# Hybrid decoder trunk: weight sums of the feed-forward by accumulating transfers, three plain tiles, and four smaller edits

## Chip, cores and metric

The kernel runs on one core of a Trainium2 chip. The metric is the device time of one execution in microseconds (us). Before the change the median of 3 runs is 1248.66 us, from 1247.74 to 1249.43. PE is the matrix engine (its weight loads are listed as PEld), DVE the vector engine, ACT the scalar engine, POOL the GpSimd engine, and SP the queue that issues nearly all DMA transfers.

## The reference

Two layers, each an attention part of three head groups followed by a SwiGLU feed-forward, on 512 tokens of width 1024 with a hidden width of 2816:

```python
for l in range(DEPTH):
    h = rms_norm(x, attn_norm[l])
    proj = h @ w_in[l]
    ...                       # forgetting, differential and top-k sparse attention
    x = x + concatenate([o_fox, o_diff, o_dsa]) @ w_out[l]
    h = rms_norm(x, ffn_norm[l])
    gate, up = split(h @ w_gate_up[l], 2)
    x = x + (silu(gate) * up) @ w_down[l]
```

All inputs and outputs are float32.

## The kernel before

Activations are kept transposed: eight tiles `x[m]` of 128 features by 512 tokens. Every large product is made of three matrix passes: each operand is split into a rounded part `h` (written by ACT) and a remainder `lo` (written by DVE, in the projections of attention mostly by POOL), and `mm3` (lines 165 to 168) adds h*h, lo*h and h*lo. So PE never reads a raw weight: SP loads it, ACT rounds it, DVE subtracts, and only then PE starts.

The feed-forward (`feed_forward`, line 936) handles the hidden width in 22 tiles of 128 columns, `f` = 0 to 21. For `f` below `DIRECT` (4) a tile is plain: gate and up are each eight k-tiles by three passes of 512 columns, 48 matmuls. From `f` = 4 on a tile goes through `seven` (line 1026): the 2 by 2 block product of gate and up against the two halves of the tokens and of the features, by seven instead of eight half-size products (Winograd's form), 7 x 4 x 3 = 84 matmuls of 256 columns. Its products run in the order a11, T2, T3, T1, a12, T4, 22; the second ones on a bank (a12, T4, 22) add to what the first ones left there, so DVE or ACT must have read the bank before. For it `input_sums` (line 994) makes sums of the normalized input's quarters once a layer, and each tile needs four sums of weight quarters, `ws_f_0` to `ws_f_3`, which DVE makes (lines 1036 to 1039) from two raw tiles of 512 KB. `split_sum` (line 1017) then splits each sum, `whole` the three quarters that are used as they are. The sums and the temporaries of `input_sums` share one ring of five buffers (tag `ws`); the split sums have rings of five each. `down` (line 1086) follows after f = 7, f = 14 and at the end.

The order of PE's work is the order in which the code is written. The other engines' order is set by a scheduler with the priorities of `AHEAD`, and each engine then runs its list strictly in that order; so an instruction that waits holds up everything behind it on its engine. POOL has no work in the feed-forward.

Outside the feed-forward the change touches `key_stacks` (line 423), which makes the two stacked transposes of a key's rounded part and remainder on PE, with an ACT copy each; the first load (line 112); and the last add and store of `down` (lines 1095 to 1097).

Of the kernel before, what the change touches and what calls it, by code (L numbers as in the profile page):

```python
# [11 lines left out]
F32 = mybir.dt.float32  # L12
F32R = mybir.dt.float32r
AF = mybir.ActivationFunctionType
ALU = mybir.AluOpType
AX = mybir.AxisListType

P = 128
S = 512
NB = S // P  # L20
D = 1024
KT = D // P
DEPTH = 2
# [3 lines left out]
NF = FF // P  # L27
# [28 lines left out]


VALUES = [4, 4, 2, 4, 4, 2]
DIRECT = 4
GH = 8  # L60
POFF = (0, 512, 896, 1152)

# [24 lines left out]
def trunk(ctx: ExitStack, tc: tile.TileContext, x_in, w_in, w_out, w_gu, w_dn, vecs, gfeat, rope, out):  # L87
    nc = tc.nc
    V, A, G, T, SY = nc.vector, nc.scalar, nc.gpsimd, nc.tensor, nc.sync
# [4 lines left out]
    small = ctx.enter_context(tc.tile_pool(name="small", bufs=2))  # L94
# [11 lines left out]
    f32 = lambda ap: ap.bitcast(F32)  # L106
# [2 lines left out]

    x = [main.tile([P, S], F32, name=f"x{m}") for m in range(KT)]  # L110
    gf = const.tile([P, gfeat.shape[1]], F32, name="gf")
    SY.dma_start(gf, gfeat)


    ident = const.tile([P, P], F32, name="ident")
# [105 lines left out]
    def attention(l, ap):  # L221
# [189 lines left out]
        def stacked(src, name, tag="qk", bufs=5):  # L411

            ps = st_tile(f"tp_{name}", F32R)
            for b in range(NB):
                T.transpose(ps[:, b * P:(b + 1) * P], src(b), identr)
            dst = ap.tile([P, S], F32R, tag=tag, name=f"T_{name}", bufs=bufs)
            with ahead("stack"):
                A.activation(dst, ps, AF.Copy)
            return dst

        flat = lambda a: a.rearrange("p t e -> p (t e)")

        def key_stacks(hl, name, tag="qk", bufs=5):

            return [stacked(lambda b: flat(hl(b))[:, 64 * e:64 * e + 128], f"{name}{e}", tag, bufs) for e in range(2)]


        def scores(blocks, q, k, bias, p, stat, name):
# [289 lines left out]
        raws, hl, rr, outs, lows = {}, {}, {}, {}, {}  # L718
# [169 lines left out]
        q = index_queries(0)  # L888
        for h in range(IDX):
            if h == 1:  # L890
                skT = key_stacks(lambda b: hlk[:, b, 1], f"sk{l}", "skT", 2)
            step(filler, int(INDEX_FILL[4 * h + 1]))
            nq = index_queries(h + 1) if h + 1 < IDX else None
            for i in range(1, NB):
                step(filler, int(INDEX_FILL[4 * h + 1 + i]))
                index_score(h, q, i)
            q = nq
# [38 lines left out]
    def feed_forward(l, fp):  # L936
# [3 lines left out]
        y = split_input(l, 1, range(KT))  # L940
        acc = square_sum(fp, f"1{l}", (("gh", GH), ("gl", GH)))
        R = fp.tile([P, S], F32, tag="R", name=f"R{l}")
        half = KT // 2 * P
        H = S // 2

# [46 lines left out]
        Y = {}  # L992

        def input_sums(kt):
            xg = []
            for m in (kt, kt + KT // 2):
                t = fp.tile([P, S], F32, tag="ws", name=f"xg{l}_{m}", bufs=5)
                A.activation(t, x[m], AF.Copy, scale=gf[:, (2 * l + 1) * KT + m:(2 * l + 1) * KT + m + 1])
                xg.append(t)
            b11, b12, b21, b22 = (t[:, o:o + H] for t in xg for o in (0, H))  # L1000
            ta, tb = (fp.tile([P, S], F32, tag="ws", name=f"t{i}{l}_{kt}", bufs=5) for i in "ab")
            t1, t3, t2, t4 = (t[:, o:o + H] for t in (ta, tb) for o in (0, H))
            V.tensor_tensor(t1, b12, b11, op=ALU.subtract)
            V.tensor_tensor(t3, b22, b12, op=ALU.subtract)
            V.tensor_tensor(t2, b22, t1, op=ALU.subtract)
            V.tensor_tensor(t4, b21, t2, op=ALU.subtract)
            Y[kt] = {k: [t[:, o:o + H] for t in y[m]] for k, m, o in
                     (("11", kt, 0), ("21", kt + KT // 2, 0), ("22", kt + KT // 2, H))}
            for src, name, ks in ((ta, "s", ("T1", "T3")), (tb, "t", ("T2", "T4"))):
                h = fp.tile([P, S], F32R, tag=f"Yh{name}{kt}", name=f"Yh{l}_{name}{kt}")  # L1010
                A.activation(h, src, AF.Copy)
                lo = fp.tile([P, S], F32R, tag=f"Yl{name}{kt}", name=f"Yl{l}_{name}{kt}")
                V.tensor_tensor(lo, src, f32(h), op=ALU.subtract)
                for i, k in enumerate(ks):
                    Y[kt][k] = [t[:, i * H:(i + 1) * H] for t in (h, lo)]
# [10 lines left out]
        def seven(f):  # L1026

            raws, parts = [], {}
            for u in range(2):
                raw = (fp if u else wp).tile([P, 1024], F32, tag="raw", name=f"raw_gu{l}_{f}_{u}", bufs=2)  # L1030
                SY.dma_start(raw, w_gu[l, :, (2 * f + u) * KT * P:(2 * f + u + 1) * KT * P])
                raws.append(raw)
            a11, a12, a21, a22 = (r[:, o:o + half] for r in raws for o in (0, half))
            sums = [fp.tile([P, half], F32, tag="ws", name=f"ws{l}_{f}_{i}", bufs=5) for i in range(4)]
            with ahead("fh"):
                V.tensor_tensor(sums[0], a21, a22, op=ALU.add)
                V.tensor_tensor(sums[1], sums[0], a11, op=ALU.subtract)
                V.tensor_tensor(sums[2], a11, a21, op=ALU.subtract)
                V.tensor_tensor(sums[3], a12, sums[1], op=ALU.subtract)

            def whole(src, k):
                h = wp.tile([P, 512], F32R, tag="wh", name=f"wh_gu{l}_{f}_{k}")
                with ahead("fh"):
                    A.activation(h, src, AF.Copy)
                lo = wp.tile([P, 512], F32R, tag="wl", name=f"wl_gu{l}_{f}_{k}")
                with ahead("fl"):
                    V.tensor_tensor(lo, src, f32(h), op=ALU.subtract)
                return h, lo

            def product(ps, w, k, first, last):  # L1050
                for kt in range(KT // 2):
                    cs = slice(kt * P, (kt + 1) * P)
                    mm3(ps, w[0][:, cs], w[1][:, cs], *Y[kt][k], first and kt == 0, last and kt == KT // 2 - 1)

            a, c = (mm_tile(f"gu{l}_{f}_{k}")[:, :H] for k in "ac")
            b, d = (st_tile(f"gu{l}_{f}_{k}")[:, :H] for k in "bd")
            gs, us = pair(f)
            u2 = fp.tile([P, H], F32, tag="u2", name=f"u2{l}_{f}", bufs=2)
            product(a, whole(a11, "a"), "11", True, True)
            with ahead("post"):  # L1060
                A.activation(u2, a, AF.Copy)
            product(b, split_sum(sums[1], f"{l}_{f}_1", V), "T2", True, True)
            with ahead("post"):
                V.tensor_tensor(u2, b, u2, op=ALU.add)
            product(d, split_sum(sums[2], f"{l}_{f}_2", V), "T3", True, True)
            with ahead("post"):
                V.tensor_tensor(us[:, H:], d, u2, op=ALU.add)
            product(c, split_sum(sums[0], f"{l}_{f}_0", V), "T1", True, True)
            with ahead("post"):
                V.tensor_tensor(us[:, H:], c, us[:, H:], op=ALU.add)  # L1070
            product(a, whole(a12, "b"), "21", False, True)
            with ahead("post"):
                V.tensor_tensor(gs[:, :H], a, R[:, :H], op=ALU.mult)
            product(d, whole(a22, "d"), "T4", False, True)
            with ahead("post"):
                V.tensor_tensor(us[:, :H], d, u2, op=ALU.add)
            V.tensor_tensor(us, us, R, op=ALU.mult)
            product(c, split_sum(sums[3], f"{l}_{f}_3", V), "22", False, True)
            with ahead("post"):
                V.tensor_tensor(gs[:, H:], c, u2, op=ALU.add)  # L1080
            V.tensor_tensor(gs[:, H:], gs[:, H:], R[:, H:], op=ALU.mult)
            A.activation(gs, gs, AF.Silu)
            V.tensor_tensor(us, us, gs, op=ALU.mult)
            inner(f, us)

        def down(group, ms):
            f0, f1 = DOWN_GROUPS[group]
            n = (f1 - f0) * P
            for m in ms:
                off = KT * P * f0 + m * n  # L1090
                part = weights(w_dn[l, :, off:off + n], n, P, f"dn{l}_{f0}_{m}", low="fl")
                ps = mm_tile(f"dn{l}_{f0}_{m}")
                for e, f in enumerate(range(f0, f1)):
                    mm3(ps, *part(e * P, (e + 1) * P), gt[f][0], gt[f][1], f == f0, f == f1 - 1)
                V.tensor_tensor(x[m], ps, x[m], op=ALU.add)  # L1095
                if l == DEPTH - 1 and f1 == NF:
                    SY.dma_start(out[:, m, :], x[m])

        def norm_row():
            rows = st_tile(f"rrow{l}")  # L1100
# [96 lines left out]
```

## Time and profile before

| | |
|---|---|
| median of 3 runs | 1248.66 us |
| the profiled execution's own time | 1247.4 us |
| its span, first to last instruction | 1245.7 us |
| PE busy / DVE busy / ACT busy / POOL busy | 99% / 80% / 60% / 21% |
| PE's share of the chain that ended last | 91% |
| mean granted clock of PE | 1.00 |
| feed-forward of layer 0 / layer 1 | about 278 to 616 us / 895 to 1242 us |

Busy shares are means over stages with different limits: in the tiles of the seven-product form PE and DVE are both full, in `down` DVE has room. The profile lists each instruction's start and duration; neighbouring instructions of one engine overlap, so the cost of one in a full row of them is the distance between two starts, not its duration.

### The profile page before, as it was taken

The numbers are of one execution on the slowest core, as the hardware profiler recorded it, in microseconds if no ns is written. First come the engines' busy times: TensorE is split into PE (matmuls) and PEld (weight loads), VectorE is DVE, ScalarE is ACT, GpSimd is POOL, SyncE is SP. The second block draws the span as 40 slices with busy tenths as digits, with TensorE's granted clock in tenths as the row PEclk, the third lists the DMA queues.
The fourth block names the chain that finished last, engine by engine and source line by source line (L and its number), as shares of the span: only waits on it lengthen the run. The fifth ranks groups of instructions, "written<-read, shape, count | busy, mean of one in ns | idle before, by whom it ended". The sixth has DMA issues, their size and how long they took to land.

```text
span 1245.7 us, 22873 instructions
## 1 busy us (share of the span) xinstructions
PE 1230.3 (99%) x8366; PEld 1112.1 (89%) x8366; DVE 1001.2 (80%) x2345; ACT 741.9 (60%) x1686; POOL 262.2 (21%) x379
## 2 busy tenths in 40 slices
PE   9999999999999999999999899999999999999998
PEld 9988897887998998999899888978789989989997
DVE  5689987879976995998545999868799679959962
ACT  6678778867543552554457787888675335534531
POOL 2554566320000000000026635653200000000000
PEclk9999999999999999999999999999999999999999
DMA  5221221133423332422332312211333243234232
GB/s 191 86 77 52 77 74 35 57 109 102 117 77 112 116 99 81 130 85 69 98 89 69 94 52 60 74 47 52 119 102 114 77 131 102 82 99 125 75 97 83
DMA packets 34640, 111.77 MB, mean 90 GB/s; under 512 B 3952, under 2 KB 4448, under 8 KB 34528
## 3 DMA queue, kind: packets, MB, share of 16 engines
q1 hardware_dynamic: 34528, 110.31, 29.7%
q8 instruction: 66, 1.08, 0.4%
q14 instruction: 46, 0.38, 0.1%
HBM read 108.14 MB, written 2.15 MB: 89 GB/s over the span
## 4 chain that ended last, share of the span: by engine, by line
PE 91%; DVE 5%; ACT 3%; issue 0%; DMA 0%; SPq 0%; ACTq 0%; DVEq 0%
PE dn L168 7%; PE dn L167 6%; PE dn L166 6%; PE pj L166 6%; PE pj L168 6%; PE pj L167 6%; PE gu_d L166 3%; PE gu_a L166 3%; PE gu_a L167 3%; PE gu_d L168 3%; PE gu_a L168 3%; PE gu_d L167 3%; PE gu_c L166 3%; PE gu_c L167 3%; PE gu_c L168 3%; PE gu L166 2%
## 5 line engine op out<-in xcount | busy, mean ns | idle before, releaser
L166 PE MATMUL pj<-wh_in,yh 128*128 128x256 f32 (+1 forms) x704 | 201.8, 287 | 1.3 <-ACT wh_in L151 1.3
L168 PE MATMUL pj<-wl_in,yh 128*128 128x256 f32 (+1 forms) x704 | 198.5, 282 | 0.2 <-DVE wl_in L156 0.2
L167 PE MATMUL pj<-wh_in,yl 128*128 128x256 f32 (+1 forms) x704 | 198.4, 282 | 0.0
L151 ACT ACTIVATE wh_dn<-raw_dn 128x512 fp32r<-128x512 f32 x96 | 57.1, 595 | 138.6 <-PE dn L168 106.3
L168 PE MATMUL dn<-gl,wh_dn 128*128 128x512 f32 x352 | 138.7, 394 | 0.0
L167 PE MATMUL dn<-gh,wl_dn 128*128 128x512 f32 x352 | 138.0, 392 | 0.0
L166 PEld LDWEIGHTS pj<-wh_in,yh 128*128 128x128 f32 x704 | 134.3, 191 | 4.0 <-issue 1.9
L166 PE MATMUL dn<-gh,wh_dn 128*128 128x512 f32 x352 | 136.6, 388 | 0.0
L167 PEld LDWEIGHTS pj<-wh_in,yl 128*128 128x128 f32 x704 | 134.4, 191 | 0.7
L168 PEld LDWEIGHTS pj<-wl_in,yh 128*128 128x128 f32 x704 | 134.4, 191 | 0.4 <-DVE wl_in L156 0.4
L156 POOL TENSOR_TENSOR wl_in<-raw_in,wh_in 128x256 fp32r<-128x256 f32 x144 | 107.5, 774 | 112.3 <-ACT wh_in L151 85.0
L1020 ACT ACTIVATE wsh<-ws 128x512 fp32r<-128x512 f32 x144 | 89.5, 630 | 68.8 <-PE gu_c L168 29.3
L156 DVE TENSOR_TENSOR wl_dn<-raw_dn,wh_dn 128x512 fp32r<-128x512 f32 x96 | 61.6, 645 | 49.6 <-ACT wh_dn L151 49.0
L1023 DVE TENSOR_TENSOR wsl<-ws,wsh 128x512 fp32r<-128x512 f32 x144 | 97.6, 684 | 0.7
L167 PEld LDWEIGHTS dn<-gh,wl_dn 128*128 128x128 f32 x352 | 66.1, 188 | 15.2
L166 PEld LDWEIGHTS dn<-gh,wh_dn 128*128 128x128 f32 x352 | 66.1, 188 | 14.5
L168 PEld LDWEIGHTS dn<-gl,wh_dn 128*128 128x128 f32 x352 | 66.2, 188 | 13.1
L231 POOL MEMSET causal<- 128x512 f32 x2 | 1.1, 527 | 357.8 <-PE dn L168 357.8
L1095 DVE TENSOR_TENSOR x<-dn,x 128x512 f32<-128x512 f32 x48 | 32.8, 690 | 43.8 <-PE dn L168 43.7
L151 ACT ACTIVATE wh_in<-raw_in 128x512 fp32r<-128x512 f32 (+1 forms) x88 | 53.4, 623 | 20.8 <-PE pj L167 11.4
L880 DVE MAX8 top<-sc 128x8 f32<-128x384 f32 (+2 forms) x96 | 51.7, 547 | 0.3
L881 DVE MATCH_REPLACE8 sc<-top,sc 128x384 f32<-128x384 f32 (+2 forms) x96 | 51.5, 538 | 0.0
(397 smaller groups left out, 3935.6 us busy)
## 6 DMA issues: line engine op xcount, KB each, us to landing
raw_gu<-in_w_gu SPq DMA_DIRECT2D x88, 512.0 KB
raw_in<-in_w_in SPq DMA_DIRECT2D x39, 512.0 KB
raw_dn<-in_w_dn SPq DMA_DIRECT2D x32, 448.0 KB
raw_dn<-in_w_dn SPq DMA_DIRECT2D x16, 512.0 KB
cr<-rtd_c SPq DMA_DIRECT2D x12, 256.0 KB
raw_o_fox<-in_w_out SPq DMA_DIRECT2D x8, 384.0 KB
x<-in_x_in SPq DMA_DIRECT2D x8, 256.0 KB
raw_o_diff<-in_w_out SPq DMA_DIRECT2D x4, 512.0 KB
```

The source lines that it names most:

```text
L151: A.activation(h[:, :w], raw[:, o:o + w], AF.Copy)
L156: eng.tensor_tensor(lo[:, a:e], raw[:, o + a:o + e], f32(h[:, a:e]), op=ALU.subtract)
L166: T.matmul(ps, ah, bh, start=first, stop=False, skip_group_check=True)
L167: T.matmul(ps, al, bh, start=False, stop=False, skip_group_check=True)
L168: T.matmul(ps, ah, bl, start=False, stop=last, skip_group_check=True)
L231: G.memset(causal, 0.0)
L880: V.max(top, sc[i])
L881: V.match_replace(sc[i], top, sc[i], TAKEN)
L1020: A.activation(h, src, AF.Copy)
L1023: eng.tensor_tensor(lo, src, f32(h), op=ALU.subtract)
L1095: V.tensor_tensor(x[m], ps, x[m], op=ALU.add)
```

## The change

Six edits in one.

1. `DIRECT` is 3: tile f = 3 of each layer goes through `seven` too.
2. In `seven`, `ws_f_0` (a21 + a22) and `ws_f_2` (now a11 + a21) are made by the DMA engines: POOL issues a plain load of one quarter from memory into the buffer, waits for it, and issues a second load that adds to it. DVE makes `ws_f_1` and `ws_f_3` alone. The signs that this turns are put right in the input sums, in one add and in the multiply by `R`, which becomes a scalar_tensor_tensor.
3. `input_sums` scales one tile instead of two on ACT and scales the other inside DVE's instructions, with a negated copy of the scale (`gneg`).
4. The second of the two stacks of the sparse heads' key is copied from the first by two SP transfers that swap the halves of the partitions, instead of four transposes and an ACT copy.
5. The first load (`gf`) is issued by ACT instead of SP.
6. The last tile's add and store are made in two halves of 256 tokens.

```diff
-DIRECT = 4
+DIRECT = 3
...
-    SY.dma_start(gf, gfeat)
+    A.dma_start(gf, gfeat)
...
+            second = ap.tile([P, S], F32R, tag=tag, name=f"T_{name}1", bufs=bufs)
+            SY.dma_start(f32(second[0:64]), f32(first[64:128]))
+            SY.dma_start(f32(second[64:128]), f32(first[0:64]))
...
-                skT = key_stacks(lambda b: hlk[:, b, 1], f"sk{l}", "skT", 2)
+                skT = key_stacks(lambda b: hlk[:, b, 1], f"sk{l}", "skT", 2, True)
...
-            for m in (kt, kt + KT // 2):
-                t = fp.tile([P, S], F32, tag="ws", name=f"xg{l}_{m}", bufs=5)
-                A.activation(t, x[m], AF.Copy, scale=gf[:, (2 * l + 1) * KT + m:(2 * l + 1) * KT + m + 1])
-                xg.append(t)
...
+            A.activation(xg, x[kt], AF.Copy, scale=gf[:, c:c + 1])
+            V.tensor_tensor(t1, xg[:, :H], xg[:, H:], op=ALU.subtract)
+            V.scalar_tensor_tensor(t3, b22, g, xg[:, H:], op0=ALU.mult, op1=ALU.subtract)
+            V.scalar_tensor_tensor(t2, b22, g, t1, op0=ALU.mult, op1=ALU.add)
+            V.scalar_tensor_tensor(t4, b21, ng, t2, op0=ALU.mult, op1=ALU.add)
...
+            for i, (p, q) in ((0, (2, 3)), (2, (0, 2))):
+                blocks = [w_gu[l, :, (2 * f * KT + k * KT // 2) * P:(2 * f * KT + (k + 1) * KT // 2) * P] for k in (p, q)]
+                G.dma_start(sums[i], blocks[0])
+                G.dma_start(sums[i], blocks[1], accum_op=ALU.add)
             with ahead("fh"):
-                V.tensor_tensor(sums[0], a21, a22, op=ALU.add)
-                V.tensor_tensor(sums[1], sums[0], a11, op=ALU.subtract)
-                V.tensor_tensor(sums[2], a11, a21, op=ALU.subtract)
-                V.tensor_tensor(sums[3], a12, sums[1], op=ALU.subtract)
+                V.tensor_tensor(sums[1], sums[0], a11, op=ALU.add)
+                V.tensor_tensor(sums[3], a12, sums[1], op=ALU.add)
...
-                V.tensor_tensor(u2, b, u2, op=ALU.add)
+                V.tensor_tensor(u2, u2, b, op=ALU.subtract)
...
-            V.tensor_tensor(us, us, R, op=ALU.mult)
+            V.scalar_tensor_tensor(us, us, -1.0, R, op0=ALU.mult, op1=ALU.mult)
...
+                last = l == DEPTH - 1 and f1 == NF
+                w = S // 2 if last and m == KT - 1 else S
+                for o in range(0, S, w):
+                    V.tensor_tensor(x[m][:, o:o + w], ps[:, o:o + w], x[m][:, o:o + w], op=ALU.add)
+                    if last:
+                        SY.dma_start(out[:, m, o:o + w], x[m][:, o:o + w])
```

POOL's list in the feed-forward of layer 0 is empty before. After the change it holds 76 transfers a layer; here are those of tiles 12 and 13. `ws_12_0` is sum 0 of tile 12, and the bracket names the semaphores that the transfer waits for (DMASW: another transfer of POOL's).

```order
L1045 DMA ws_12_0_6157<-in_w_gu 128x512 [waits DVE_49]
L1046 DMA ws_12_0_6157<-in_w_gu 128x512 [waits DMASW4_49]
L1045 DMA ws_12_2_6159<-in_w_gu 128x512 [waits DMASW7_49,DMASW6_49,DVE_49]
L1046 DMA ws_12_2_6159<-in_w_gu 128x512 [waits DMASW6_49]
L1045 DMA ws_13_0_6305<-in_w_gu 128x512 [waits DVE_49]
L1046 DMA ws_13_0_6305<-in_w_gu 128x512 [waits DMASW1_49,DMASW0_49]
```

Each adding transfer waits until the plain one has landed, and stands ahead of everything else on POOL. In tiles 11 to 14 and 18 to 21 the four transfers of a tile stand in this order; in the others both plain ones come first.

DVE's list in the middle of tile 11, before: the sums of tile 13 stand among the reads of tile 11's banks (`gu_11_d`, `gu_11_c`) and the remainders of tile 12 (`wsl_12`).

```order
L1036 TENSOR_TENSOR ws_13_0_6229<-raw_gu_13_1_6227 128x512
L1070 TENSOR_TENSOR us_11_5950<-gu_11_c,us_11_5950 128x256
L1023 TENSOR_TENSOR wsl_12_3_6203<-ws_12_3_6086,wsh_12_3_6201 128x512
L1037 TENSOR_TENSOR ws_13_1_6230<-ws_13_0_6229,raw_gu_13_0_6225 128x512
L1073 TENSOR_TENSOR gs_11_5949<-gu_11_a,R_4232 128x256
```

The same place after the change:

```order
L1077 TENSOR_TENSOR us_11_6024<-gu_11_d,u_11_6025 128x256
L1048 TENSOR_TENSOR ws_13_1_6306<-ws_13_0_6305,raw_gu_13_0_6301 128x512
L1030 TENSOR_TENSOR wsl_12_0_6227<-ws_12_0_6157,wsh_12_0_6225 128x512
L1080 TENSOR_TENSOR us_11_6024<-gu_11_c,us_11_6024 128x256
L1030 TENSOR_TENSOR wsl_12_3_6279<-ws_12_3_6160,wsh_12_3_6277 128x512
```

The first sum is gone from DVE; the second now waits for the transfers of `ws_13_0`, and the read of tile 11's bank `gu_11_c` stands behind it.

## Rows read from the trace of the kernel before

**Rows 1.** The page: busy time of each engine, and the chain's shares.
```profile
PE 1230.3 (99%) x8366; PEld 1112.1 (89%) x8366; DVE 1001.2 (80%) x2345; ACT 741.9 (60%) x1686; POOL 262.2 (21%) x379
PE 91%; DVE 5%; ACT 3%; issue 0%; DMA 0%; SPq 0%; ACTq 0%; DVEq 0%
```

**Rows 2.** Windows: start:end, length, busy of each engine, clock, DMA share, GB/s.
```profile
324.80:334.75 9.95, 9.95 (x86) 9.95 (x84) 9.95 (x20) 5.22 (x9) 0.00 (x0) 1.00 0.35 107
334.75:344.70 9.95, 9.95 (x86) 9.95 (x85) 9.95 (x20) 5.23 (x9) 0.00 (x0) 1.00 0.35 99
500.00:600.00 100.00, 100.00 (x722) 94.54 (x722) 89.89 (x167) 49.42 (x85) 0.00 (x0) 1.00 0.33 95
```

**Rows 3.** Waits of PE: who waited for whom, us in total, times, longest.
```profile
PE rt_c L496 <- DVE cum L759: 2.4, 2, 1.2
PE s_d L438 <- DVE st_d L444: 2.0, 4, 0.8
```

**Rows 4.** Timeline of PE: first matmul of tiles 2, 4, 5 and 6.
```profile
302.93 0.48 PE L166 MATMUL gu<-yh,wh_gu 128*128 128x512 f32 x1
...
324.80 0.28 PE L166 MATMUL gu_a<-yh,wh_gu_a 128*128 128x256 f32 x1
...
334.75 0.28 PE L166 MATMUL gu_a<-yh,wh_gu_a 128*128 128x256 f32 x1
...
344.70 0.28 PE L166 MATMUL gu_a<-yh,wh_gu_a 128*128 128x256 f32 x1
```

**Rows 5.** Timeline of PE: the second key stack's transposes and what follows.
```profile
54.10 0.80 PE L415 MATMUL tp_sk<-identr,hlik 128*128 128x128 f32 x8
54.73 0.25 PE L415 MATMUL tp_iq<-identr,hliq 128*128 128x128 f32 x1
```

**Rows 6.** Timeline of all engines at the start.
```profile
0.81 1.28 ACT L1129 ACT_TABLE_LOAD   x1 [0.81 <-PEq L1189]
0.81 0.39 SPq L112 DMA_DIRECT2D gf<-in_gfeat  x1
...
1.26 0.42 SPq L188 DMA_DIRECT2D x<-in_x_in  x1
...
2.71 0.15 DVE L310 TENSOR_SCALAR dg<-gf 128x1 f32<-128x1 f32 x1 [1.76 <-DMA gf<-in_gfeat]
...
4.52 0.72 ACT L192 ACTIVATE yh<-x,gf 128x512 fp32r<-128x512 f32 x1 [2.43 <-DMA x<-in_x_in]
```

**Rows 7.** Timeline of all engines: the last add and the last store.
```profile
1242.06 0.69 DVE L1095 TENSOR_TENSOR x<-dn,x 128x512 f32<-128x512 f32 x1 [4.80 <-PE dn L168]
1242.78 0.33 SPq L1097 DMA_DIRECT2D out_x<-x  x1
```

**Rows 8.** Windows: the last store's data, then a 512 KB load before and in its data.
```profile
1243.62:1244.44 0.82, 0.00 (x0) 0.00 (x0) 0.00 (x0) 0.00 (x0) 0.00 (x0) 1.00 0.83 317
...
301.44:302.40 0.96, 0.96 (x6) 0.80 (x5) 0.96 (x3) 0.04 (x1) 0.00 (x0) 1.00 0.00 0
302.40:304.64 2.24, 2.24 (x14) 1.85 (x13) 2.10 (x4) 1.83 (x4) 0.00 (x0) 1.00 0.79 234
```

**Rows 9.** Timeline of DVE in tile 5: distances between starts.
```profile
338.48 0.68 DVE L1037 TENSOR_TENSOR ws<-ws,raw_gu 128x512 f32<-128x512 f32 x1
339.07 0.69 DVE L1023 TENSOR_TENSOR wsl<-ws,wsh 128x512 fp32r<-128x512 f32 x1
339.68 0.42 DVE L1067 TENSOR_TENSOR us<-gu_d,u 128x256 f32<-128x256 f32 x1
340.01 0.68 DVE L1023 TENSOR_TENSOR wsl<-ws,wsh 128x512 fp32r<-128x512 f32 x1
```

**Rows 10.** Timeline of DVE and PE before and in the first seven-product tile.
```profile
302.61 0.69 DVE L1013 TENSOR_TENSOR Yl_s<-ta,Yh_s 128x512 fp32r<-128x512 f32 x1
...
307.04 0.68 DVE L988 TENSOR_TENSOR us<-us,gs 128x512 f32<-128x512 f32 x1
...
331.96 0.28 PE L166 MATMUL gu_d<-Yh_t,wh_gu_d 128*128 128x256 f32 x1
```

More of the change, by code (lines that the diff above doesn't have):

```diff
@@ L421, in attention, with key_stacks @@
         flat = lambda a: a.rearrange("p t e -> p (t e)")
-        def key_stacks(hl, name, tag="qk", bufs=5):
-            return [stacked(lambda b: flat(hl(b))[:, 64 * e:64 * e + 128], f"{name}{e}", tag, bufs) for e in range(2)]
+        def key_stacks(hl, name, tag="qk", bufs=5, swap=False):
+            first = stacked(lambda b: flat(hl(b))[:, 0:128], f"{name}0", tag, bufs)
+            if not swap:
+                return [first, stacked(lambda b: flat(hl(b))[:, 64:192], f"{name}1", tag, bufs)]
+            second = ap.tile([P, S], F32R, tag=tag, name=f"T_{name}1", bufs=bufs)
+            SY.dma_start(f32(second[0:64]), f32(first[64:128]))
+            SY.dma_start(f32(second[64:128]), f32(first[0:64]))
+            return [first, second]
         def scores(blocks, q, k, bias, p, stat, name):
@@ L942, in feed_forward @@
         R = fp.tile([P, S], F32, tag="R", name=f"R{l}")
+        gneg = small.tile([P, KT // 2], F32, tag="gneg", name=f"gneg{l}")
+        G.tensor_scalar(gneg, gf[:, (2 * l + 1) * KT + KT // 2:(2 * l + 2) * KT], -1.0, None, op0=ALU.mult)
         half = KT // 2 * P
@@ L994, in input_sums @@
         def input_sums(kt):
-            xg = []
-            for m in (kt, kt + KT // 2):
-                t = fp.tile([P, S], F32, tag="ws", name=f"xg{l}_{m}", bufs=5)
-                A.activation(t, x[m], AF.Copy, scale=gf[:, (2 * l + 1) * KT + m:(2 * l + 1) * KT + m + 1])
-                xg.append(t)
-            b11, b12, b21, b22 = (t[:, o:o + H] for t in xg for o in (0, H))
+            c = (2 * l + 1) * KT + kt
+            g, ng = gf[:, c + KT // 2:c + KT // 2 + 1], gneg[:, kt:kt + 1]
+            b21, b22 = (x[kt + KT // 2][:, o:o + H] for o in (0, H))
             ta, tb = (fp.tile([P, S], F32, tag="ws", name=f"t{i}{l}_{kt}", bufs=5) for i in "ab")
+            xg = fp.tile([P, S], F32, tag="ws", name=f"xg{l}_{kt}", bufs=5)
             t1, t3, t2, t4 = (t[:, o:o + H] for t in (ta, tb) for o in (0, H))
[L1003 to L1006, printed above, removed]
+            A.activation(xg, x[kt], AF.Copy, scale=gf[:, c:c + 1])
[3 more added lines that the diff above has]
+            V.scalar_tensor_tensor(t4, b21, ng, t2, op0=ALU.mult, op1=ALU.add)
             Y[kt] = {k: [t[:, o:o + H] for t in y[m]] for k, m, o in
@@ L1094, in down @@
                     mm3(ps, *part(e * P, (e + 1) * P), gt[f][0], gt[f][1], f == f0, f == f1 - 1)
-                V.tensor_tensor(x[m], ps, x[m], op=ALU.add)
-                if l == DEPTH - 1 and f1 == NF:
-                    SY.dma_start(out[:, m, :], x[m])
+                last = l == DEPTH - 1 and f1 == NF
[4 more added lines that the diff above has]
+                        SY.dma_start(out[:, m, o:o + w], x[m][:, o:o + w])
         def norm_row():
```

## The prediction

> **What bounds the kernel now.** I read the page first: PE is busy 99% of the span, DVE 80%, ACT 60%, and PE holds 91% of the chain that ended last [rows 1]. Then the windows of two tiles of the seven-product form and of a long stretch of the feed-forward: in a tile PE and DVE are both full for all 9.95 us, and from 500 to 600 us PE is busy all the time while DVE has 10 us left over, in `down` [rows 2]. PE's clock is at 1.00 there, so no clock is to be won. Then PE's waits: the longest stand in attention and are a few us in all [rows 3]. So in the feed-forward nothing counts but the length of PE's own list. Relief for DVE is worth nothing by itself, but DVE must not become late, because PE follows it without slack in the tiles.
>
> **The change part by part.** Durations are of the profiled execution (1247.4 us, 1.3 below the median of the runs); I add the sum to the median at the end.
>
> *Tile 3 through the seven products.* Plain tiles 2 and 3 take 324.80 - 302.93 = 21.87 us, 10.935 each; a seven-product tile takes 9.95 [rows 4]. That is 0.985 less per layer, **-1.97** for two. It is paid only if PE is not held up there.
>
> *Key stack.* The eight transposes of both stacks run from 54.10 to 54.73, so four take 0.32 [rows 5]; two layers: **-0.63**. The copy that the transfers replace is needed only some products later. If PE reaches the wait on `cum` earlier [rows 3], the gain is eaten there: between -0.63 and 0.
>
> *First load.* `x` is issued at 1.26 because `gf` takes 0.39 of the queue from 0.81; ACT's first work on `x` is at 4.52 and waits for `x` [rows 6]. With `gf` on ACT the load of `x` starts at 0.81: **-0.45**. ACT's table load, 1.28 long, slides behind the 0.39 and ends near 2.5, still before `x`. The cover goes only if `gf` lands over 1.4 us later than now.
>
> *Tail.* The last add takes 0.69, the store's issue follows at once, and the last data move for 0.82 [rows 7, 8]. In halves the first store starts some 0.3 earlier; the second add ends about 0.07 later (a 256-wide one is 0.34 in a full row, a 512-wide 0.60 [rows 9]) and its issue waits some 0.1 behind the first; but the last data are half, 0.41 less. About **-0.3**, between -0.5 and +0.1.
>
> *Input sums, `gneg`, the sign in the multiply.* One ACT pass less per k-tile, POOL is idle in the feed-forward [rows 2], and a few instructions of equal width on DVE. Nothing on PE's path; their cover is the 9.95 us tile, and its loss is in the first-tile term below.
>
> *DVE per tile.* Before, 14 wide at 0.60 and 7 narrow at 0.34 make 10.8 [rows 9], more than 9.95: DVE falls behind and makes it up in `down`. Without two wide ones it is 9.6, less than PE's tile. Worth nothing itself, but it lets DVE stay ahead.
>
> *The accumulating transfers in the loop.* Here a wait is added, and behind it stands all of DVE's list: `ws_13_1` waits for the transfers of `ws_13_0`, and the read of `gu_11_c`, which PE's product 22 of tile 11 needs, stands two instructions behind. The buffer of `ws_13_0` is freed by the remainder of sum 3 of tile 11. From there POOL does a plain transfer and an adding one, one after the other; call that C. Then DVE needs `ws_13_1` to `wsl_12_3`, three wide and one narrow, 2.2 us [rows 9], and the ring turns again. So the period is C + 2.2, and PE never waits as long as C is under 9.95 - 2.2 = 7.75. No row before shows a transfer issued by POOL nor one that adds, so I bound C. A 256 KB store was through 1.66 us after its issue (1242.78 to 1244.44) [rows 7, 8]: two of them, 3.3, are the low end. A 256 KB load's waiter ran 3.26 us after its issue (`x`, 1.26 to 4.52, seven others beside it) [rows 6]; a 512 KB load needed 0.96 + 2.24 = 3.2 [rows 8], and I take the adding transfer as that, since it also reads the buffer. That gives 3.26 + 3.2, **C = 6.5**, the value I take. High end: both meet a whole raw load, 2 x 2.24 more, 10.9; the raw loads take two such stretches, 4.5 of each 9.95 us. The DMA share of 0.35 [rows 2] rises by as much again for the four transfers (1 MB, like the raw tiles) and by up to half of that for the second read: 0.70 to 0.88, full enough to collide, not full. At C = 6.5 the loop has 1.2 us to spare: **0**.
>
> A page speaks to this price in both directions. The Trainium skill, "DMA: Bandwidth & Descriptors", section "Anatomy of one DMA — SWDGE (gpsimd) path", gives a transfer issued by POOL a fixed 2.0 us plus its bytes at 436 GB/s; an estimate from it is 2.6 us each and C = 5.2, by which the loop has 2.5 us to spare. A load of 512 KB moved at 234 GB/s in the trace [rows 8], about half of the page's rate.
>
> *The first tile of this form.* Tile 3 now starts at 302.93 + 10.94 = 313.87 instead of 324.80, and its product T4, 7.16 us into the tile (331.96 before) [rows 4, 10], comes at 321.03. From where `us<-us,gs` stood (307.04) DVE's new list has 20 wide and one narrow before the read that frees T4's bank: 12.3 us, so that this read runs from 319.4 to 319.8. So 1.2 us are left. But the sums of tiles 3 and 4 take buffers which the temporaries of `input_sums` give back, the last at 302.61 + 0.69 = 303.3 [rows 10]; `ws_3_2` is then there at 309.8 with C = 6.5, and DVE wants its rounded form near 309.6, after 0.6 of ACT. A wait of 0.9 takes the slack. With C at the low end nothing is lost, with 10.9 about 4 us a layer. I take 0.25 per layer: **+0.5**.
>
> Sum: -1.97 - 0.63 - 0.45 - 0.3 + 0.5 = -2.85. On the profiled execution 1244.55, on the median of 1248.66 **1245.8 us**. Outside the span lie 1.7 us, which I leave as they are, though a new queue of transfers could move them by some tenths.
>
> **The rivals.** About 0.2%, 2.5 us, is what a measurement of this kernel can tell from no change; the limits are 1246.2 and 1251.2.
>
> 1. *The transfers set the pace of the loop* (slower). Place: DVE's wait for `ws_f_0` in tiles 11 to 14 and 18 to 21, eight a layer, sixteen in all, where the four transfers stand in single file. It decides from C = 7.75 on. If the adding transfer costs one more load's data (2.24), C is 8.7, the period 10.9, and 16 tiles lose 0.95 each; about 2 us in each of the four runs of tiles are absorbed, since T1's bank is read 2 us before 22 needs it. That is +7: 1253. At C = 10.9 it is 3.15 x 16 - 8 = +42: 1288. For it: every step is a round trip through memory, the DMA engines will be over 70% busy, and DVE runs in strict order. Against it: the 1.2 us to spare and DVE's lighter list. Chance 0.24.
>
> The Trainium skill, "Collectives: The Full Stack", section "The bandwidth ceiling: the fold count and why AG ≠ RS ≠ AR", says that an add in the DMA engines reads two sources and so runs at half the rate of a copy; this rule speaks for this rival, and no run so far shows an adding transfer. By it the data part of the adding transfer is that of a 512 KB load, which is what I took in C, and 8.7 needs more than the rule.
>
> 2. *The start of the feed-forward stalls* (same). The loop keeps pace, but each of the first transfers is 1 us later than I took, with the 512 KB loads of tile 4 in the same engines; the read before T4 moves by 2 us, 1 us past T4, and PE loses about 1.8 instead of 0.25 per layer: +3.1, 1248.9. For it: the slack worked out above is near nothing, and PE gets there 11 us earlier than before. Against: DVE could have idle time before 307 to work ahead. Chance 0.21.
>
> 3. *The small gains are absorbed* (same). Key stack, start and tail give nothing (1.4 us): 1247.2. For it: the waits of PE on DVE in attention are there already [rows 3]. Against: PE's own list at 99%, where each instruction less should show. Chance 0.10.
>
> **How the numbers follow.** The forecast has 0.45, and its own range is 1244.8 to 1246.8 (the tail's and the key stack's bounds, the first-tile term from 0 to 1). Faster by over 0.2% comes from about 0.38 of it and 0.01 of rival 3: 0.39. Within: 0.07, 0.09, 0.18 of rival 2 and 0.02 of rival 1: 0.36. Slower: the rest of rival 1 and 0.03 of rival 2: 0.25. The range must take in rivals 2 and 3 and the near part of rival 1: 1244.5 to 1259.
>
> **What would show it.** Right: PE still busy all of 500 to 600 us; tile 3 of the seven-product form with starts 9.95 apart; DVE under 10 us a tile, with short waits for `ws` on DMA or none that PE follows; `x` issued near 0.81 and ACT's first work near 4.07; no second key stack on PE; a DMA share of 0.70 to 0.88 in the tiles. The forecast is wrong if tiles 11 to 14 are longer than 9.95 with DVE waiting for `ws_f_0` (rival 1), if PE stands before T4 or 22 of tiles 3 and 4 (rival 2), or if waits in attention grow by what the transposes gave (rival 3). The time from one sum to the next on POOL's queue measures C directly.

## Result and profile after

The changed kernel takes 1324.53 us in the median (1319.68 to 1326.0, 4 runs) against 1248.20 for the one before (4 runs): a ratio of 1.060 with a 95% interval from 1.0587 to 1.0612, 76 us slower. The profiled run spans 1324.3 us. The forecast was 1245.8, and its rival 1, the transfers setting the pace, gave 1253 to 1288. The mechanism is that rival's, but it was priced too low, and about half of the loss stands in tiles that it did not name.

The page shows PE no longer full, and the chain going through the new transfers (to compare with [rows 1]). First PE's row, then the chain's shares by engine and by line:

```profile
PE 1260.0 (95%) x8430; PEld 1138.5 (86%) x8430; DVE 974.5 (74%) x2296; ACT 735.2 (56%) x1684; POOL 372.4 (28%) x533
...
PE 56%; issue 17%; DMA 15%; DVE 7%; ACT 3%; POOL 2%; SPq 0%; DVEq 0%; POOLq 0%; ACTq 0%
DMA ws<-in_w_gu 14%; PE pj L166 6%; PE pj L167 5%; PE pj L168 5%; PE dn L168 3%; PE dn L166 3%; PE dn L167 3%; PE o_d L488 1%; PE o_f L488 1%; PE gu_c L166 1%; POOL ws L1045 1%; PE s_f L444 1%; PE s_s L444 1%; POOL ws L1046 1%; PE gu_c L167 1%
```

PE's two largest groups of waits are now in the feed-forward (who waited for whom, us in total, times, longest): before T4 (`gu_d`) and before product 22 (`gu_c`), in both cases for DVE's read of the bank. Before, the largest group was 2.4 us in two waits, in attention [rows 3].

```profile
PE gu_d L166 <- DVE us L1077: 28.1, 9, 4.5
PE gu_c L166 <- DVE us L1080: 21.0, 9, 3.8
```

The windows of tiles 9 to 13 and then of the whole group of seven tiles (start:end, length, busy of PE, PEld, DVE, ACT, POOL, clock, DMA share, GB/s; compare [rows 2]):

```profile
425.91:435.94 10.03, 10.03 (x86) 10.03 (x85) 7.89 (x16) 5.75 (x10) 2.86 (x4) 1.00 0.70 180
435.94:448.15 12.21, 10.30 (x87) 10.10 (x85) 9.17 (x20) 5.63 (x10) 2.85 (x4) 1.00 0.68 170
448.15:463.49 15.34, 11.51 (x87) 11.30 (x86) 10.85 (x22) 5.63 (x10) 2.85 (x4) 0.85 0.65 153
463.49:474.52 11.03, 11.03 (x85) 11.03 (x85) 9.11 (x19) 5.74 (x10) 2.86 (x4) 0.90 0.63 162
474.52:484.56 10.04, 10.04 (x86) 10.04 (x85) 10.01 (x21) 5.56 (x10) 1.44 (x2) 1.00 0.80 201
410.00:494.60 84.60, 74.64 (x589) 74.03 (x588) 62.81 (x124) 36.17 (x64) 17.16 (x24) 0.94 0.66 163
```

Two things are to be seen. A group of seven takes 84.6 us where seven tiles without a wait take 70.3 (7 x 10.04). PE is idle for 10.0 of the 14.3 that are lost; the other 4.3 go mostly in work at the lower of its two clocks. Tile 11 has a wait of 3.8 us, and the granted clock of tiles 11 and 12 is 0.85 and 0.90; tile 10, with a wait of 1.9, keeps 1.00. And even a tile without any wait (9, 13) takes 10.04 instead of the 9.95 of [rows 4]; that is a second loss, which nothing in the prediction foresaw.

DVE's list around the read that PE waits for in tile 11 (start, duration; in brackets the idle time ahead). The two `ws` rows are the second sums of tiles 12 and 13:

```profile
444.94 0.69 DVE L1048 TENSOR_TENSOR ws<-ws,raw_gu 128x512 f32<-128x512 f32 x1 [3.04 <-issue]
...
446.49 0.68 DVE L1030 TENSOR_TENSOR wsl<-ws,wsh 128x512 fp32r<-128x512 f32 x1
...
454.17 0.42 DVE L1077 TENSOR_TENSOR us<-gu_d,u 128x256 f32<-128x256 f32 x1
459.08 0.69 DVE L1048 TENSOR_TENSOR ws<-ws,raw_gu 128x512 f32<-128x512 f32 x1 [4.49 <-issue]
...
460.29 0.42 DVE L1080 TENSOR_TENSOR us<-gu_c,us 128x256 f32<-128x256 f32 x1
```

POOL's transfers in the same stretch (L1045 plain, L1046 adding):

```profile
447.47 0.57 POOL L1045 DMA_DIRECT2D ws<-in_w_gu  x1 [0.66 <-DVE wsl L1030]
451.87 0.86 POOL L1046 DMA_DIRECT2D ws<-in_w_gu  x1 [3.83 <-DMA ws<-in_w_gu]
452.41 0.89 POOL L1045 DMA_DIRECT2D ws<-in_w_gu  x1
459.89 0.86 POOL L1046 DMA_DIRECT2D ws<-in_w_gu  x1 [6.59 <-DMA ws<-in_w_gu]
```

And PE's product 22 of tile 11 behind it:

```profile
460.76 0.58 PE L166 MATMUL gu_c<-yh,wsh 128*128 128x256 f32 x1 [3.83 <-DVE us L1080]
461.14 0.41 PE L167 MATMUL gu_c<-yh,wsl 128*128 128x256 f32 x1
461.35 0.41 PE L168 MATMUL gu_c<-yl,wsh 128*128 128x256 f32 x1
```

This is the ring of the prediction, link by link. DVE's remainder ends at 447.17 (446.49 + 0.68) and frees the buffer; POOL issues the plain transfer at 447.47 and, held by its landing, the adding one at 451.87; DVE goes on at 459.08. The bracket of that row names no releaser; that DVE waited for the adding transfer follows from its list, where `ws_13_1` needs `ws_13_0`. So C is 11.9 here, and with 2.2 us of DVE's work the period is the 14.14 between the two `ws` rows. This is the longest of the sixteen such periods (sums of tiles 11 to 14 and 18 to 21, both layers): they go from 11.06 to 14.14, and DVE stands waiting in thirteen of them. The mean is 12.4, so C is 10.2 in the mean. PE's matmuls after the wait stand 0.21 apart instead of 0.12: 1.2 GHz instead of 2.4.

The largest waits stand elsewhere, before T4 in the first tile after a `down`. Here POOL's transfers for tile 10's first sum, DVE's wait for them and PE's wait in tile 8:

```profile
406.60 0.87 POOL L1045 DMA_DIRECT2D ws<-in_w_gu  x1
410.86 0.55 POOL L1045 DMA_DIRECT2D ws<-in_w_gu  x1 [3.39 <-ACT wh_gu_b L1054]
412.17 0.89 POOL L1046 DMA_DIRECT2D ws<-in_w_gu  x1 [0.76 <-DMA ws<-in_w_gu]
...
420.41 0.69 DVE L1048 TENSOR_TENSOR ws<-ws,raw_gu 128x512 f32<-128x512 f32 x1 [6.06 <-DMA ws<-in_w_gu]
421.02 0.42 DVE L1077 TENSOR_TENSOR us<-gu_d,u 128x256 f32<-128x256 f32 x1
...
421.49 0.58 PE L166 MATMUL gu_d<-Yh_t,wh_gu_d 128*128 128x256 f32 x1 [4.22 <-DVE us L1077]
```

In this tile both plain transfers come first: the plain one is issued at 406.60, the adding one to the same buffer at 412.17, and DVE goes on 8.2 us after that.

Over all 76 pairs the times from issue to landing are (min/median/max at the end of each line's page):

```profile
L1045 POOL DMA_DIRECT2D ws<-in_w_gu x76: 546/573/897, 299.8 to 1247.0; - x76
...
DMA to landing us min/median/max: 2.9/4.7/7.8
```
```profile
L1046 POOL DMA_DIRECT2D ws<-in_w_gu x76: 856/862/1132, 303.3 to 1253.1; - x76
...
DMA to landing us min/median/max: 4.1/5.1/8.2
```

The small edits did what they were to do. `x` is issued at 0.82 and ACT works on it at 4.00 instead of 4.52 [rows 6], and the second key stack is gone: four transposes in place of the eight of [rows 5].

```profile
0.82 0.39 SPq L188 DMA_DIRECT2D x<-in_x_in  x1
...
4.00 0.72 ACT L192 ACTIVATE yh<-x,gf 128x512 fp32r<-128x512 f32 x1 [1.47 <-DMA gf<-in_gfeat]
...
54.91 0.46 PE L415 MATMUL tp_sk<-identr,hlik 128*128 128x128 f32 x4
...
1320.48 0.76 DVE L1108 TENSOR_TENSOR x<-dn,x 128x256 f32<-128x256 f32 x2 [4.89 <-PE dn L168]
```

The bracket of the second row shows one cover that went: ACT's first work now waits for `gf`, no longer for `x`. DVE's first reader of `gf` starts at 4.00 too, against 2.71 before [rows 6].

### The profile page after: what moved, and what is told of

It reads as the page before. It is cut to its first block, busy times and chain, and to the rows that moved or that the text cites. A ratio compares the mean times of both kernels' runs of the same rounds, so it can differ in the third digit from the quotient of the medians.

```text
span 1324.3 us, 23271 instructions
## 1 busy us (share of the span) xinstructions
PE 1260.0 (95%) x8430; PEld 1138.5 (86%) x8430; DVE 974.5 (74%) x2296; ACT 735.2 (56%) x1684; POOL 372.4 (28%) x533
## 4 chain that ended last, share of the span: by engine, by line
PE 56%; issue 17%; DMA 15%; DVE 7%; ACT 3%; POOL 2%; SPq 0%; DVEq 0%; POOLq 0%; ACTq 0%
DMA ws<-in_w_gu 14%; PE pj L166 6%; PE pj L167 5%; PE pj L168 5%; PE dn L168 3%; PE dn L166 3%; PE dn L167 3%; PE o_d L488 1%; PE o_f L488 1%; PE gu_c L166 1%; POOL ws L1045 1%; PE s_f L444 1%; PE s_s L444 1%; POOL ws L1046 1%; PE gu_c L167 1%
## 5 line engine op out<-in xcount | busy, mean ns | idle before, releaser
L1045 POOL DMA_DIRECT2D ws<-in_w_gu x76 | 53.6, 706 | 328.0 <-DVE wsl L1030 241.9
L1046 POOL DMA_DIRECT2D ws<-in_w_gu x76 | 66.6, 879 | 222.1 <-DMA ws<-in_w_gu 211.5
L1030 DVE TENSOR_TENSOR wsl<-ws,wsh 128x512 fp32r<-128x512 f32 x152 | 102.7, 683 | 5.2 <-ACT wsh L1027 4.6
L1048 DVE TENSOR_TENSOR ws<-ws,raw_gu 128x512 f32<-128x512 f32 x38 | 26.3, 692 | 92.1 <-DMA ws<-in_w_gu 49.6
L166 PE MATMUL gu_d<-Yh_t,wh_gu_d 128*128 128x256 f32 x152 | 46.3, 304 | 28.1 <-DVE us L1077 28.1
L166 PE MATMUL gu_c<-yh,wsh 128*128 128x256 f32 x152 | 48.1, 317 | 21.0 <-DVE us L1080 21.0
```

What stands on the lines that cost most here:

```text
L166: T.matmul(ps, ah, bh, start=first, stop=False, skip_group_check=True)
L1030: eng.tensor_tensor(lo, src, f32(h), op=ALU.subtract)
L1045: G.dma_start(sums[i], blocks[0])
L1046: G.dma_start(sums[i], blocks[1], accum_op=ALU.add)
L1048: V.tensor_tensor(sums[1], sums[0], a11, op=ALU.add)
```

## Experiments

Ratios are to the kernel before, with 95% intervals. All of them belong to one question: what do the transfers cost, and what is the rest?

**1. All sums by DVE.**

```diff
-                G.dma_start(sums[i], blocks[0])
-                G.dma_start(sums[i], blocks[1], accum_op=ALU.add)
+                V.tensor_tensor(sums[0], a21, a22, op=ALU.add)
+                V.tensor_tensor(sums[2], a11, a21, op=ALU.add)
```

> The changed kernel with all four weight sums made by DVE again, everything else of the change left in. Theory A (the loss is the accumulating transfers alone): all of the +76 us goes, and what is left is the sum of the other terms of the prediction without its first-tile cost, -3.3, so about 1245. Rival (the feed-forward's buffers, moved by 64 bytes in SBUF by the new tile of the negated scale, make PE's matmuls longer: in the changed kernel a matmul of the last product 22 starts every 118.6 ns instead of 114.7, one of down every 232.2 instead of 228.7): 1,056 x 3.5 ns + 456 x 4 ns and some more, about +6, so about 1250. Rival (other edits of the change cost tens of us): above 1260.

1264.42 us, 1.0134 (1.0118 to 1.0149). Most of the loss goes, so it is the transfers'. But 16 us stay, which is above 1260, the third theory's side: other edits cost too, and experiments 5 and 12 say which. PE waits 7.6 us before T4 in four of the first tiles, and a tile without a wait takes 10.04.

```profile
PE gu_d L166 <- DVE us L1075: 7.6, 4, 3.0
```

**2. The same with the scale's tile padded.**

```diff
-        gneg = small.tile([P, KT // 2], F32, tag="gneg", ...)
+        gpad = small.tile([P, 16], F32, tag="gneg", ...)
+        gneg = gpad[:, :KT // 2]
```

> As the run with DVE's sums, but the new tile of the negated scale is made 64 bytes wide instead of 16, so that the feed-forward's buffers move by 128 bytes instead of 64 against the kernel before. If the place in SBUF sets the matmuls' pace: down at about 228.7 ns a matmul again, 5 to 7 us less than the run without the padding, near 1244. If not: the same time as without the padding, and the pace is due to something else.

1261.92 us, 1.0099 (1.0085 to 1.0114): 2.5 less, not 5 to 7. A tile now takes 9.89, less than before the change, but `down` 39.19, more than with the shift of 64 (39.04). So 128 bytes do not bring the old pace back: one kind of product got shorter, the other longer.

```profile
410.39:420.28 9.89, 9.89 (x85) 9.89 (x84) 9.53 (x18) 4.70 (x8) 0.00 (x0) 1.00 0.38 121
371.20:410.39 39.19, 39.19 (x171) 31.59 (x170) 23.82 (x39) 12.51 (x22) 0.00 (x0) 1.00 0.33 107
```

**3. Both transfers plain** (the adding is left out).

```diff
-                G.dma_start(sums[i], blocks[1], accum_op=ALU.add)
+                G.dma_start(sums[i], blocks[1])
```

> The changed kernel, but the second transfer of each sum is a plain load too: the adding is left out, so the sums are wrong. Theory A1 (two transfers in a row through POOL's queue are slow, whatever they do; a plain one took 4.7 us from issue to landing in the median, an adding one 5.1): C goes from about 11 to 10 or so, and the time falls by less than a third of the loss, to 1300 to 1320. Rival A2 (the adding, which reads its target, is what is slow): most of the loss goes, below 1270.

1259.39 us, 1.009 (1.0068 to 1.0112). Theory A1 falls and A2 holds as stated: the adding is a large part. The medians are 3.8 and 3.9 us, together 7.7, and PE's waits in the tiles shrink from 49.1 to 2.9 us in the profiled executions. First the plain transfer, then the one that was adding:

```profile
DMA to landing us min/median/max: 2.8/3.8/5.9
```
```profile
DMA to landing us min/median/max: 2.8/3.9/5.7
```

**4. No raw loads beside them** (all seven-product tiles of a layer use the first one's weights).

```diff
-                SY.dma_start(raw, w_gu[l, :, ...])
+                if u not in held:
+                    held[u] = fp.tile([P, 1024], F32, tag="raw", ...)
+                    SY.dma_start(held[u], w_gu[l, :, ...])
```

> The changed kernel, but the two raw tiles of 512 KB are loaded once a layer instead of once for each seven-product tile (all those tiles use the same weights, so the output is wrong); the transfers of POOL stay as they are. Rival A3 (the transfers are slow because SP's loads of 512 KB are in the same DMA engines): the transfers land in 3 to 4 us, C is below 7.75, the loss goes: about 1250. Theory A1 (the path through POOL's queue by itself): C stays above 9, and the time above 1285.

1262.82 us, 1.0116 (1.0102 to 1.0129). A1 falls here too. A3 has the time nearly right, but not the landing, which stays above 4 us in the median, first the plain, then the adding transfer:

```profile
DMA to landing us min/median/max: 2.8/4.1/6.1
```
```profile
DMA to landing us min/median/max: 3.8/4.2/5.7
```

So the collision with SP's loads is a large part too. Runs 3 and 4 don't contradict each other: the loss is what lies over a limit, and either brings C back near it.

**5. The kernel before with an unread tile of 16 bytes.**

```diff
+        shift = small.tile([P, KT // 2], F32, tag="shift", name=f"shift{l}")
+        G.memset(shift, 0.0)
```

> The kernel before, with nothing changed but a new tile of 16 bytes (two buffers, 64 bytes with the rounding) in the pool that lies ahead of the feed-forward's, written once a layer by POOL and read by nobody. Theory P (where the feed-forward's buffers lie in SBUF sets the distance of matmuls): the pace of the changed kernel appears here too, down 39.0 instead of 38.5 us for 168 matmuls, a seven-product tile 10.04 instead of 9.95, so 1,056 x 3.5 ns + 36 x 90 ns = +7, about 1255. Rival (the slower pace comes with the other work of the changed kernel): 1248, no difference.

1254.86 us, 1.0055 (1.0042 to 1.0067): theory P, to 0.2 us. The windows of tile 8 and of the first `down` in this kernel, whose feed-forward does the same work as before:

```profile
404.22:414.26 10.04, 10.04 (x86) 10.03 (x85) 9.65 (x19) 4.70 (x8) 0.00 (x0) 1.00 0.41 140
365.18:404.22 39.04, 39.04 (x170) 31.66 (x169) 23.60 (x39) 12.72 (x22) 0.00 (x0) 1.00 0.32 102
```

The same two in the kernel before:

```profile
403.06:413.01 9.95, 9.95 (x85) 9.95 (x84) 9.47 (x19) 4.70 (x8) 0.00 (x0) 1.00 0.48 151
364.61:403.06 38.45, 38.45 (x170) 31.55 (x169) 23.54 (x39) 12.72 (x22) 0.00 (x0) 1.00 0.35 102
```

PE is busy throughout at the full clock in both; only the distance of its matmuls has grown. That is a cost of `gneg`, which I had put at nothing. The bytes of the shift are counted from the sizes of the buffers; no view shows an address.

**6. The three small edits alone** (key stack, first load, last store, word for word as in the change).

> The kernel before with three of the six edits: the swapped key stack, the first load on ACT, the last store in halves. By the terms of the prediction -0.63 - 0.45 - 0.3 = -1.4: 1246.7. Rival (they are absorbed by waits): 1248.1. Nothing else moves in SBUF in the feed-forward.

1247.21 us, 0.9992 (0.9983 to 1.0001). The gain, 0.8 of the 1.4, is inside what can't be told from nothing. The transposes' part is there (0.29 from the start of the remaining four to the next work), but ACT's first work comes at 4.40, only 0.12 earlier: it waits for `gf` here too.

**7. A ring of their own for the accumulated sums.**

```diff
-            ... tag="ws", name=f"ws{l}_{f}_{i}", bufs=5) for i in range(4)]
+            ... tag="ws" if i % 2 else "wa", ..., bufs=3 if i % 2 else 4) for i in range(4)]
```

> The changed kernel, but the two accumulated sums of a tile have a ring of four buffers of their own, and DVE's two sums one of three (the ring of the remainders of the sums is cut from five to four to make room). So the transfers of a tile wait for the sums of the tile two before, and no longer for DVE's. Theory R (the transfers are only started too late, the ring of five is what makes C count): C of 10 fits into the lead of a tile, most of the loss goes, about 1265. Rival (the path of the transfers itself is full: POOL's queue or the DMA engines): more than half of the loss stays, above 1285.

1279.74 us, 1.0252 (1.0236 to 1.0268): 45 of the 76 us come back, but it is still 20 slower than experiment 3. An earlier start helps, but doesn't hide the path; the result lies between the two theories. The shorter ring of the remainders is in this run too, and its share isn't known.

**8. One sum by transfers, three by DVE.**

```diff
-            for i, (p, q) in ((0, (2, 3)), (2, (0, 2))):
+            for i, (p, q) in ((2, (0, 2)),):
```

> The changed kernel, but only one of the two sums (a11 + a21) is made by transfers, DVE makes the other three. Half of POOL's transfers go, and with them the single file. If the loss comes from the sum of both pairs in one queue and one ring (C over 7.75): nearly all of it goes, and DVE with 13 wide and 7 narrow instructions (10.2 us a tile) is nearly full: 1255 to 1262. If one adding transfer that lands late is enough: above 1280.

1261.91 us, 1.0108 (1.0092 to 1.0123), at the upper end of what was expected. One pair a tile lands in 3.0 and 4.5 us in the median, and the single file is gone. With experiment 1 at 1264.42, nothing is left of the transfers' loss.

**9. The small edits with a pad of 128 bytes behind R.**

```diff
+        pad = fp.tile([P, 32], F32, tag="pad", name=f"pad{l}")
+        G.memset(pad, 0.0)
```

> The kernel before with the three small edits (key stack, first load, last store), and a tile of 128 bytes behind R in the feed-forward's pool: the gated tiles gh and gl stay where they are, the weight sums, input sums and what follows move by 128 bytes. In the run with the padded scale, where all moved by 128, a seven-product tile took 9.90 instead of 9.95 us, but down 39.2 instead of 38.5. If the place decides each product by itself: tiles of 9.90 and down of 38.5, so 36 x 0.05 = 1.8 less than the small edits alone, 1245.4. Rival (what matters is the place of all together): no gain, 1247 or more.

1245.93 us, 0.9982 (0.9973 to 0.9990): faster than both kernels, by 2.3 us against the one before. Against experiment 6 the two intervals overlap, so the time alone doesn't show what the pad gives; the windows do. Tile 8 takes 9.90 and `down` its old 38.46:

```profile
402.88:412.78 9.90, 9.90 (x85) 9.90 (x84) 9.53 (x18) 4.70 (x8) 0.00 (x0) 1.00 0.38 129
364.42:402.88 38.46, 38.46 (x171) 31.56 (x169) 23.66 (x39) 12.70 (x22) 0.00 (x0) 1.00 0.34 108
```

**10. The transfers alone** (with their input sums; DIRECT 4, nothing moved in SBUF).

```diff
-DIRECT = 3
+DIRECT = 4
...
-        gneg = small.tile([P, KT // 2], F32, tag="gneg", name=f"gneg{l}")
+        gneg = small.tile([P, KT // 2], F32, tag="ls", name=f"gneg{l}", bufs=1)
```

> The kernel before with the accumulating transfers and the input sums that go with them alone: DIRECT is 4, key stack, first load and last store are as before, and the negated scale takes an idle tile of the same size, so that nothing moves in SBUF. Theory (the loss is the transfers, C + 2.2 over a tile's 9.95 us): the groups of seven tiles after each down take 84 to 85 us instead of 69.8 again, +59 for four of them and less in the first groups: 1305 to 1318. Rival (the earlier start at tile 3 or the place in SBUF carries a large part): below 1290.

1304.30 us, 1.0447 (1.0427 to 1.0467): 56 us by themselves, just under the expected range. A tile without a wait takes 9.95 here. PE waits 42.2 us in the tiles:

```profile
PE gu_c L166 <- DVE us L1074: 27.5, 14, 4.0
PE gu_d L166 <- DVE us L1071: 14.7, 4, 4.5
```

**11. One plain and one adding transfer a tile that nobody waits for.**

```diff
+            probe = fp.tile([P, half], F32, tag="probe", name=f"probe{l}_{f}", bufs=1)
+            G.tensor_scalar(probe[:, 0:1], us[:, 0:1], 1.0, None, op0=ALU.mult)
+            ... G.dma_start(probe, block) ... G.dma_start(probe, block, accum_op=ALU.add)
```

> The kernel before, and beside it one plain and one adding transfer of 256 KB for each seven-product tile into a buffer that nobody reads; a one-column POOL instruction starts each pair when the tile is done. This measures the two transfers by themselves, beside the raw loads, with no ring and no waiter, at half of the changed kernel's traffic. Theory (C is a property of the path): plain 3 to 4 us from issue to landing, adding 4 to 5, together 8 and more, more where a raw load is in flight. My price in the prediction: 3.3 and 3.2. The time: 1248 if only waits cost, more if the traffic alone delays SP's loads.

1248.72 us, 1.0001 (0.9992 to 1.0010): half of the changed kernel's traffic costs nothing that can be measured when nobody waits for it. From issue to landing, first the plain, then the adding one:

```profile
DMA to landing us min/median/max: 2.8/3.0/3.8
```
```profile
DMA to landing us min/median/max: 3.9/4.9/7.4
```

**12. DIRECT = 3 alone.**

```diff
-DIRECT = 4
+DIRECT = 3
```

> The kernel before with DIRECT = 3 alone, the sums by DVE as before. The term of the prediction by itself: -2.0, 1246. Rival (DVE can't have the first tiles' work done by then: in the run with DVE's sums PE stood 7.6 us in all before T4 in the first group of tiles, and a first group took 56.6 instead of 50.2): +9 to +11, about 1258.

1258.08 us, 1.0073 (1.0060 to 1.0085): the term that I had at -2.0 is +9.8 by itself. In tile 3 PE waits 2.9 us for DVE, and its granted clock in the tile is 0.88; DVE is busy for 13.31 of the 14.66 us:

```profile
314.06:328.72 14.66, 11.76 (x85) 11.55 (x84) 13.31 (x25) 6.38 (x12) 0.00 (x0) 0.88 0.24 80
```

## Why the prediction was wrong

Each part alone, against the kernel before:

| part | predicted | measured |
|---|---|---|
| accumulating transfers (10) | 0 in the loop | +56 |
| DIRECT = 3 (12) | -2.0, with first-tile cost -1.5 | +9.8 |
| place in SBUF (5) | not seen | +6.8 |
| key stack, first load, last store (6) | -1.4 | -0.8 |
| sum | -2.9 | +72 of +76 |

The missing 4 us are about what the intervals of the parts leave open, and the parts can act on each other; no run isolates that. In experiment 12 DVE makes the sums, so its +9.8 is not the same stall as in the changed kernel. Without the transfers the sum holds better: 9.8 + 6.8 - 0.8 = 15.8 against 16.3 in experiment 1.

**The step that failed is C.** The mechanism and its limit of 7.75 were right, and C + 2.2 gives the measured period. C itself was taken as 3.26 + 3.2 = 6.5, with 1.2 us to spare; it is 10.2 in the mean of the sixteen periods and 11.9 in the longest. The price of the plain transfer was right for a pair by itself (3.0). That of the adding one was not: I took it as a 512 KB load, because it reads as much, and with no other pair in POOL's queue it takes 4.9. With that one number, and the 0.3 from DVE's remainder to POOL's issue, C is 3.0 + 0.3 + 4.9 = 8.2, already over the limit, though by the sum of rival 1 the 2 us absorbed in each run of tiles would still cover it. The second and larger error was to price each transfer as if its pair were alone: there are two pairs a tile in POOL's one queue, and the medians become 4.7 and 5.1, with 4.4 and 7.2 in the longest ring. Without SP's raw loads they are still 4.1 and 4.2 (4), with one pair a tile 3.0 and 4.5 (8). My high end of 10.9 was meant for the case that both transfers meet a whole raw load; the mean is nearly there.

The Trainium skill, "Collectives: The Full Stack", section "The bandwidth ceiling: the fold count and why AG ≠ RS ≠ AR", says of the add in a collective that it needs two reads. The order agrees here: the fastest adding transfer took 3.9 us against 2.8 of the fastest plain one in experiment 11; what an adding transfer reads, no run shows. The estimate of 2.6 us from the Trainium skill, "DMA: Bandwidth & Descriptors", section "Anatomy of one DMA — SWDGE (gpsimd) path", is missed by 0.2 us by the fastest plain transfer and by 1.3 by the fastest adding one.

**The rival's price and its place.** With C = 10.2 the sum of rival 1 gives (10.2 - 7.75) x 16 - 8 = +31. By the starts of the tiles in the trace, the tiles in which the sums of 11 to 14 and 18 to 21 are waited for, and the one behind them (9 to 13 and 16 to 20 of both layers), are together 33.9 us longer than 10.04 each. That the two agree is in part luck: PE waits 21.0 us there, less than the sum says, and the rest is mostly work with matmuls 0.21 apart, which I had not priced. What the rival lacked is the rest of the loss, before T4: the first tile of each group of seven (8 and 15) adds 23.3 us in all, and tiles 3 to 7 of both layers 17.4, of which rival 2 named the beginning. Behind the start I had looked for the wait only where the four transfers stand in single file; in the rows of tile 8, where both plain ones come first, the adding transfer is just as late.

**The first tile.** The prediction had the read before T4 of tile 3 start at 319.4, and a wait of 0.9 for which the slack of 1.2 was enough. It started at 323.42:

```profile
307.80 0.69 DVE L1048 TENSOR_TENSOR ws<-ws,raw_gu 128x512 f32<-128x512 f32 x1 [1.06 <-DMA ws<-in_w_gu]
...
318.26 0.69 DVE L1048 TENSOR_TENSOR ws<-ws,raw_gu 128x512 f32<-128x512 f32 x1 [3.12 <-DMA ws<-in_w_gu]
...
323.42 0.42 DVE L1077 TENSOR_TENSOR us<-gu_d,u 128x256 f32<-128x256 f32 x1
...
323.89 0.39 PE L166 MATMUL gu_d<-Yh_t,wh_gu_d 128*128 128x256 f32 x1 [3.00 <-DVE us L1077]
```

The count of instructions was right: DVE lost 1.06 and 3.12 us to two `ws`, together 4.2, and 319.4 + 4.2 is that time to 0.2. Here the ring's second round (tile 4's sums) was late, which I had not followed: the adding transfer to `ws_4_0` was issued at 311.13, behind the plain one of `ws_4_2`, which had waited for a buffer until 310.60. Where DVE makes the sums instead (12), it has no such wait and is late all the same, having two more wide instructions a tile: 13.31 busy of the 14.66 us.

**Edits priced at nothing.** For `gneg` I named idle POOL as the cover, and the instruction is covered. Its buffer isn't: two buffers of 16 bytes, 64 with rounding by my count, moved the buffers of the feed-forward.

**What held:** the key stack's 0.3 a layer, `x` issued near 0.81, and in part the DMA share in the tiles (0.63 to 0.80, predicted 0.70 to 0.88).

## What to carry to other kernels

A transfer that takes work off an engine puts a round trip into a ring. Write the ring's period as round trip plus the engine's own work between, compare it with the step that it must fit into, and price the round trip with all transfers of a step in the queue, not with one alone; here 1.2 us of assumed slack was a deficit of 2.5 in the mean and of 4 at worst. A probe that nobody waits for gives such a price at no measurable cost, before anything depends on it, if it carries all the transfers of a step: the one here had a single pair and gave 8.2 where the loop had 10.2. And look for the wait at every reader of the buffer, not only where the queue is tightest. And an edit that adds a buffer, however small, is to be timed by itself with nothing else changed: it moves all that lies behind it.

## What the hardware showed unexpectedly

The distance of matmuls depends on where buffers lie in SBUF. At the full clock, 168 matmuls of 512 columns take 38.45 us with the buffers in their old place and 39.04 with them moved by 64 bytes; a tile of 84 matmuls of 256 columns takes 9.95 and 10.04 (experiment 5, with the same work). Moved by 128 they take 39.19 and 9.89 (experiment 2, with other work on DVE). With only the buffers behind R moved by 128 they take 38.46 and 9.90 (experiment 9). Over this kernel 64 bytes are worth 6.8 us. Which operands have to stand how to each other wasn't settled.

An adding transfer of 256 KB from memory took 4.9 us in the median where a plain one of the same queue took 3.0 (experiment 11, beside SP's loads). Why it takes longer wasn't settled.
